# Hybrid trunk step on one core: seven-product in-projections in two blocks of layer B instead of three, and their summed weights prepared over two blocks

## The chip, the cores and the metric

The program runs on one core of one Trainium2 chip. The metric is the device time of one execution in microseconds, as the median of three runs.

## The reference, cut to what matters

One step of a two-layer decoder trunk over a prompt of 2048 tokens and a sample batch of 8 x 8 = 64 tokens, with model width 1024. Layer A is a gated delta rule; nothing of it changes. Layer B is a retention layer:

```python
def _ret_layer(x, pos0, S0, norm_w, w_in, onorm_w, w_out):
    B, L, _ = x.shape
    p = _rmsnorm(x, norm_w) @ w_in.astype(F32)
    q, k, v, gate = jnp.split(p, [B_QK, 2 * B_QK, 2 * B_QK + B_VW], axis=-1)
    q = _rotary(q.reshape(B, L, B_HEADS, B_DK), pos0)
    k = _rotary(k.reshape(B, L, B_HEADS, B_DK), pos0) * (B_DK ** -0.5)
    v = v.reshape(B, L, B_HEADS, B_DV)
    o, S = _retention_chunked(q, k, v, S0)
    o = _rmsnorm(o, onorm_w) * jax.nn.silu(gate.reshape(B, L, B_HEADS, B_DV))
    y = x + (o.reshape(B, L, B_VW) @ w_out.astype(F32)).astype(x.dtype)
    return y, S.astype(x.dtype)
```

There are 4 heads, with q and k of 256 and v and gate of 512 columns each. The in-projection `x @ w_in` is what the change computes in another way in one block of tokens.

## The kernel before, in words

**Tiling.** The prompt is cut into four blocks of 512 tokens (n = 0 to 3), and layer B runs over block and head (h = 0 to 3). Block 0 also carries the 64 sample tokens, so its tiles are 576 columns wide. For each head the loop computes gate, q, k and v, then starts the retention of that head as a background task (`ret_prompt`, four chunks of 128 tokens, and in block 0 `ret_sample` for the sample tokens), and then does the out-projection of the head before (`flush_B`, `outproj_B`). Every float32 product is done as three float32r matmuls on a high and a low half of each operand (`PASSES`); the halves of a weight tile come from an ACT cast and a DVE subtraction (`wload`, L196 and L197).

**Two ways to the in-projection.** The direct one (`colproj`, and the loop with `pv`) is used in block 0: for a head it takes 8 column tiles of 24 matmuls, and 96 matmuls for v, that is 288 matmuls of 512 columns where a block has 512 tokens. In block 0 a column tile of 576 columns is done as two pieces of 288. The seven-product one (`quad`, `vquad`, `seven`; Strassen's scheme in Winograd's form) is used in blocks 1 to 3: for a head four quads of 7 x 12 matmuls of 256 columns, and for v 7 x 24, that is 504 matmuls of 256 columns, with sums of the products on DVE and POOL. It needs summed activations (`build_halves`, built once per block) and summed weights.

**Preparing the summed weights.** `prep(u)` makes them: two generators (u = 0 and 1), each with 24 tiles (4 heads x 6 weight groups). A tile is four loads into `Rw` (L1038), four POOL sums into `Sm` (L1040 to L1043), an ACT cast back into `Rw` (L1045), a DVE subtraction (L1046) and two stores to the scratch tensors `wh_d` (L1049, L1050). `Rw` and `Sm` of one generator are the two buffers of one tag (`ta` for u = 0, `tb` for u = 1), so the loads of the next tile wait until the stores of the last have landed. `build_halves` uses the same two tags for `T2` and `T3`.

**What sets the order.** All loads and stores go through SP's one queue, in program order. Background tasks (`_Pipe`) are generators: the main code calls `pipe.pump()` after each group of matmuls, and a generator's next part is written out once the pipe's count of matmul time has passed the number of us that it yielded. Both `prep` generators start after q and k of head 0 of block 0. At the end of block 0, `pipe.wait(*ptask)` writes out all that is left of them before `build_halves`:

```python
            yield 6.0
            ...
            yield 4.5
            ACT.copy(R, Sm)
            V.tensor_tensor(Sm.bitcast(F32R), Sm, R.bitcast(F32), op=ALU.subtract)
            yield 3.0
```

```python
            if h == 3 and n + 1 < NB:
                pipe.wait(*ptask)
                xo = build_halves(n + 1, rb)
```

A tile framework then places the instructions of each engine; an engine works through its own list in order.

Of the kernel before, what the change touches and what calls it, by code (L numbers as in the profile page):

```python
# [10 lines left out]
F32 = mybir.dt.float32  # L11
F32R = mybir.dt.float32r
AF = mybir.ActivationFunctionType
ALU = mybir.AluOpType
# [77 lines left out]
def tile_hybrid(ctx: ExitStack, tc: tile.TileContext, a: dict, S: int):  # L92
# [929 lines left out]
    def halves_of(src, vkind, u):  # L1022
# [3 lines left out]
        return [src[j][:, 512 * i + 256 * u : 512 * i + 256 * u + 256] for j in range(2) for i in range(2)]  # L1026

    def prep(u):

        pb = B.pb  # L1030
        tag = ("ta", "tb")[u]
        for h, t in ((h, t) for h in range(BH) for t in range(6)):
            src, vkind = quads(h)[t]
            R = pb.tile([128, 4, 256], F32R, tag=tag, bufs=2, name="Rw")
            Sm = pb.tile([128, 4, 256], F32, tag=tag, bufs=2, name="Sm")
            A11, A12, A21, A22 = (R[:, i, :].bitcast(F32) for i in range(4))
            for x, y in zip((A11, A12, A21, A22), halves_of(src, vkind, u)):
                nc.sync.dma_start(x, y)  # L1038
            yield 6.0
            PL.tensor_tensor(Sm[:, 0], A21, A22, op=ALU.add)  # L1040
            PL.tensor_tensor(Sm[:, 1], Sm[:, 0], A11, op=ALU.subtract)  # L1041
            PL.tensor_tensor(Sm[:, 2], A11, A21, op=ALU.subtract)
            PL.tensor_tensor(Sm[:, 3], A12, Sm[:, 1], op=ALU.subtract)  # L1043
            yield 4.5
            ACT.copy(R, Sm)  # L1045
            V.tensor_tensor(Sm.bitcast(F32R), Sm, R.bitcast(F32), op=ALU.subtract)  # L1046
            yield 3.0
            out = wh_d[h][4 * t : 4 * t + 4].rearrange("x p (l v c) -> p x l v c", l=2, v=2)[:, :, :, u, :]
            nc.sync.dma_start(out[:, :, 0], R.bitcast(F32))  # L1049
            nc.sync.dma_start(out[:, :, 1], Sm)  # L1050
            yield 4.5

# [367 lines left out]
    for n in range(NB):  # L1420
        for h in range(4):
# [16 lines left out]
            if n:  # L1438
                S_ = pb.tile([128, 2, 512], F32, tag="Sr", bufs=2, name="Sr")
                nc.sync.dma_start(S_.rearrange("p k v -> p (k v)"), sr_d[h])  # L1440
                ws = wstream(h)
                for d in (0, 2):
# [5 lines left out]
            else:  # L1448
                ahead = []
                for d in range(4):  # L1450
                    if h == 0 and d == 0:
                        ahead = colproj2([wload(a["w_qkg"][16 + 4 * h + j]) for j in range(2)], xk, width)
                    pst = ahead.pop(0) if ahead else colproj(a["w_qkg"][16 + 4 * h + d], xk, width)
                    for p, s, e in pieces(pst, 0, TB):
                        ACT.activation(GT[:, d, s:e], p, AF.Silu)
                    V.tensor_scalar(GT[:, d, :], GT[:, d, :], onB[:, h, d : d + 1], None, op0=ALU.mult)
                    (p, _, _), = pieces(pst, TB, XC)
                    ACT.activation(GTs[:, d, :], p, AF.Silu)
                    V.tensor_scalar(GTs[:, d, :], GTs[:, d, :], onB[:, h, d : d + 1], None, op0=ALU.mult)
                    pipe.pump()  # L1460
            for kind in range(2):
                pair = []
                if n == 0:
                    for j in range(2):
                        pair.append(colproj(a["w_qkg"][kind * 8 + 2 * h + j], xk, width, (pp, po)[j]))
                        pipe.pump()
# [10 lines left out]
                else:  # L1477
                    KR = dst
                if n:
                    quad(ws, xo, dst)  # L1480
                    rope_in(dst, cs[:, 0], cs[:, 1])
                else:
                    rope(pair, cs[:, 0], cs[:, 1], [(lambda s, e, j=j: dst[:, j, s:e]) for j in range(2)], 0, TB)
                    for j in range(2):
                        (p, _, _), = pieces(pair[j], TB, XC)
                        ACT.copy(raws[:, kind, j], p)
                pipe.pump()
            if start:
# [3 lines left out]
                V.tensor_copy(GTs, Gs)  # L1492
                ptask = [pipe.add(prep(u), 9, lat=9.0 * u) for u in range(2)]
            if h == 3 and n + 1 < NB:
# [13 lines left out]
            Vt = pb.tile([128, 4, 512], F32, tag="Vt", name="Vt")  # L1508
            if n:
                vquad(ws, xo, Vt)  # L1510
            else:
                S_ = pb.tile([128, 2, 512], F32, tag="Sr", bufs=2, name="Sr")
                pv = [pp("pv"), pp("pv"), pp("pv"), po("pv")]
                pvs = po("pvs")
                for kp in range(4):
                    w = wload(a["w_v"][h, kp])
                    for kk in range(2):
# [5 lines left out]
                        for c, i in order:  # L1523
                            xl, wl = PASSES[i]
                            mm(pv[c], xn[k][:, xl, c * 128 : (c + 1) * 128], w[:, wl, wk],
                               start=(k == 0 and i == 0), stop=(k == 7 and i == 2))
                        for i, (xl, wl) in enumerate(PASSES):
                            mm(pvs[:64], xn[k][:, xl, TB:XC], w[:, wl, wk],
                               start=(k == 0 and i == 0), stop=(k == 7 and i == 2))
                        pipe.pump()  # L1530
                for c in range(4):
                    ACT.copy(Vt[:, c], pv[c])
                vraw = pb.tile([128, 512], F32, tag="p2", name="vraw")[:64]
                ACT.copy(vraw, pvs[:64])
            if h == 3 and n + 1 < NB:
                pipe.wait(*ptask)
                xo = build_halves(n + 1, rb)
            end = n == NB - 1 and h == 3
# [14 lines left out]

PIN = False
LAT_E = 4.0
LAT_SUB = 51.0
# [124 lines left out]
```

## Time and profile before

| what | value |
|---|---|
| runs | 3461.81, 3466.56, 3473.41 us, median 3466.56 |
| the profiled execution | 3472.95 us |
| its span on the core | 3471.0 us |
| TensorE (PE) matmul busy | 3214.7 us, 93% |
| DVE, ACT, POOL busy | 2393.1, 1578.0, 527.7 us |
| mean granted TensorE clock | 0.97 |

The span begins with the first instruction. Layer A and its start take the first 1447 us or so; block 0 of layer B runs from there to about 2124 us, then the three seven-product blocks follow. A time in us in the rows counts from the span's start. Matmuls overlap, so the busy time of a group says less than the distance from one start to the next. A wait names the engine that waited, the line, and what ended the wait. A granted clock of 1.00 is 2.4 GHz throughout, 0.50 is 1.2 GHz throughout.

### The profile page before, as it was taken

The page shows a single profiled execution, that of the slowest core. Times are in us where ns is not written, and L with a number is a line of the kernel's source. Part 1 is how long each engine was busy: PE and PEld are TensorE (multiplying, and loading weights), DVE is VectorE, ACT ScalarE, POOL GpSimd, SP SyncE. Part 2 cuts the span into 40 slices and gives each one's busy share as a digit, 9 for nine tenths or more (in the row PEclk, how much of TensorE's full clock was granted, in tenths as well). Part 3 has the DMA queues.
Part 4 walks back from the last instruction along what each step waited for, and adds up shares of the span by engine and source line. Part 5 has one row for each costly group of instructions (what it writes and reads, how often), then busy time and mean ns, then how long its engine had stood idle before and what let it go on. Part 6 is the DMA issues. An engine that isn't in the chain of part 4 may idle for free.

```text
span 3471.0 us, 59507 instructions
## 1 busy us (share of the span) xinstructions
PE 3214.7 (93%) x21436; PEld 2812.2 (81%) x21436; DVE 2393.1 (69%) x5358; ACT 1578.0 (45%) x3607; POOL 527.7 (15%) x810
## 2 busy tenths in 40 slices
PE   7999999999999999999989837999999999999997
PEld 6999777778687788877868627889989898889996
DVE  6876877787768878557566546576676666776666
ACT  7564664465435555334334333344443344533443
POOL 1211111001100000012323240111101111111110
PEclk9999999999999999999999968999999999999999
DMA  4333544435443342467778777887677867788675
GB/s 133 94 100 109 172 125 119 131 113 146 130 131 103 87 136 81 147 200 264 247 237 263 255 251 226 274 282 249 232 253 254 278 238 242 233 278 269 222 246 170
DMA packets 429014, 669.80 MB, mean 193 GB/s; under 512 B 121760, under 2 KB 245424, under 8 KB 428720
## 3 DMA queue, kind: packets, MB, share of 16 engines
q1 hardware_dynamic: 428720, 666.01, 59.5%
q8 instruction: 169, 2.77, 0.3%
q14 instruction: 125, 1.02, 0.1%
HBM read 517.08 MB, written 146.68 MB: 191 GB/s over the span
## 4 chain that ended last, share of the span: by engine, by line
PE 58%; DVE 12%; DMA 12%; ACT 6%; POOL 4%; issue 4%; SPq 2%; POOLq 0%; DVEq 0%; ACTq 0%
PE pp L101 32%; PE sq L101 7%; PE o L101 4%; DMA w<-wh_d 3%; PE sv L101 3%; PE p L101 3%; PE kyd L101 2%; PE oT L110 1%; DVE w L197 1%; DMA wraw<-in_w_v 1%; SPq L1038 1%; DMA wraw<-in_w_qkg 1%; POOL so L587 1%; POOL Sm L1041 1%; ACT w L196 1%
## 5 line engine op out<-in xcount | busy, mean ns | idle before, releaser
L101 PE MATMUL pp<-xn,w 128*128 128x288 f32 (+1 forms) x5456 | 1106.3, 350 | 38.2 <-ACT w L196 13.5
L101 PEld LDWEIGHTS pp<-xn,w 128*128 128x128 f32 x5456 | 857.5, 191 | 149.4 <-ACT w L196 16.5
L101 PE MATMUL pp<-OG,w 128*128 128x512 f32 (+1 forms) x2880 | 599.8, 367 | 38.0 <-DVE xr L1349 23.7
L101 PEld LDWEIGHTS pp<-OG,w 128*128 128x128 f32 x2880 | 494.8, 196 | 124.0 <-DVE xr L1349 22.2
L197 DVE TENSOR_TENSOR w<-wraw,w 128x1024 fp32r<-128x1024 f32 x272 | 344.4, 1268 | 91.6 <-ACT w L196 87.2
L196 ACT CAST w<-wraw 128x1024 fp32r<-128x1024 f32 x272 | 285.5, 1052 | 260.7 <-PE pp L101 108.5
L101 PE MATMUL sq<-xn,w 128*128 128x256 f32 x2304 | 309.9, 284 | 8.7 <-DVE GT L1116 3.7
L101 PEld LDWEIGHTS sq<-xn,w 128*128 128x128 f32 x2304 | 287.8, 188 | 15.8 <-issue 7.1
L210 ACT CAST w<-wraw 128x512 fp32r<-128x512 f32 x216 | 129.4, 623 | 220.6 <-PE pp L101 77.2
L211 DVE TENSOR_TENSOR w<-wraw,w 128x512 fp32r<-128x512 f32 x216 | 148.8, 703 | 61.8 <-ACT w L210 61.2
L1349 DVE TENSOR_TENSOR xr<-xr,pp 128x512 f32<-128x512 f32 (+1 forms) x160 | 92.1, 592 | 137.0 <-PE pp L101 122.6
L743 DVE SCALAR_TENSOR_TENSOR acc<-pp,cw,acc 128x511 f32<-128x511 f32 (+2 forms) x216 | 160.7, 744 | 21.0 <-ACT acc L740 20.8
L101 PE MATMUL sv<-w,xn 128*128 128x256 f32 x1152 | 146.3, 283 | 4.8 <-DMA w<-wh_d 4.7
L101 PEld LDWEIGHTS sv<-w,xn 128*128 128x128 f32 x1152 | 141.0, 189 | 7.4 <-DVE rt L1000 3.1
L1046 DVE TENSOR_TENSOR Sm<-Sm,Rw 128x1024 fp32r<-128x1024 f32 x48 | 61.3, 1278 | 85.6 <-ACT Rw L1045 48.1
L101 PE MATMUL p<-Vh,Kt 128*128 128x512 f32 x384 | 108.1, 411 | 6.7 <-ACT Kt L1185 5.6
L488 DVE TENSOR_TENSOR VP<-VP,tm 128x66 f32<-128x66 f32 (+26 forms) x510 | 107.5, 211 | 4.4
L486 DVE TENSOR_TENSOR tm<-LP,VP 128x66 f32<-128x66 f32 (+26 forms) x510 | 105.5, 207 | 6.1 <-DMA LP<-sl 2.1
L1045 ACT CAST Rw<-Sm 128x1024 fp32r<-128x1024 f32 x48 | 50.2, 1049 | 128.5 <-POOL Sm L1043 120.3
L101 PE MATMUL o<-Sc,Qc 128*128 128x512 f32 x360 | 101.5, 405 | 7.6 <-ACT Sc L210 5.8
L1161 POOL TENSOR_TENSOR so<-oss,rsc 128x1 f32<-128x1 f32 x72 | 18.0, 250 | 591.6 <-ACT on L1159 591.5
L210 ACT CAST OG<-og 128x256 fp32r<-128x256 f32 x192 | 71.7, 405 | 62.2 <-DVE og L1225 28.9
(434 smaller groups left out, 5775.0 us busy)
## 6 DMA issues: line engine op xcount, KB each, us to landing
w<-wh_d SPq DMA_DIRECT2D x288, 512.0 KB, 5.4
wraw<-in_w_in_a SPq DMA_DIRECT2D x128, 512.0 KB, 3.6
x_d<-xr SPq DMA_DIRECT2D x160, 256.0 KB, 3.5
wraw<-in_w_qkg SPq DMA_DIRECT2D x144, 256.0 KB, 4.4
xr<-x_d SPq DMA_DIRECT2D x128, 256.0 KB, 4.1
wraw<-in_w_out_b SPq DMA_DIRECT2D x64, 512.0 KB, 4.2
wh_d<-Rw SPq DMA_DIRECT2D x48, 512.0 KB, 3.4
wh_d<-Sm SPq DMA_DIRECT2D x48, 512.0 KB, 3.6
```

Source lines behind the costliest of these rows:

```text
L101: ins = nc.tensor.matmul(out, lhsT, rhs, start=start, stop=stop)
L110: ins = nc.tensor.transpose(out, x, ident[:p, :p])
L196: ACT.copy(w[:, 0, :], raw)
L197: V.tensor_tensor(w[:, 1, :], raw, w[:, 0, :].bitcast(F32), op=ALU.subtract)
L210: ACT.copy(hi, x)
L211: V.tensor_tensor(lo, x, hi.bitcast(F32), op=ALU.subtract)
L486: V.tensor_tensor(tv, LP[:, m, m + 1 : m + 1 + n].unsqueeze(2).to_broadcast([128, n, ncol]), VP[:, m, 0:ncol].unsqueeze(1).to_broadcast([1 ...
L488: V.tensor_tensor(VP[:, m + 1 : m + 1 + n, 0:ncol], VP[:, m + 1 : m + 1 + n, 0:ncol], tv, op=ALU.subtract)
L743: V.scalar_tensor_tensor(acc[:, sh:], ap[:, : TB - sh], cw[:, ct, j : j + 1], acc[:, sh:], op0=ALU.mult, op1=ALU.add)
L1045: ACT.copy(R, Sm)
L1046: V.tensor_tensor(Sm.bitcast(F32R), Sm, R.bitcast(F32), op=ALU.subtract)
L1349: V.tensor_tensor(xs[:, s:e], xs[:, s:e], p[:, : e - s], op=ALU.add)
```

## The change

A constant `FIRST7 = 2` is the first block with seven products. Block 1 takes the direct in-projection, without the sample columns, and `build_xn` in place of `build_halves`. The wait for the prepared weights moves from the end of block 0 to the end of block 1. The yields of `prep` become about twice as long (18 to 36 us of counted matmul time for a tile), and the second generator starts 18 instead of 9 us after the first. A new helper `behind()` ties the cast and the subtraction of a tile behind the last ACT and the last DVE instruction written out before them.

```diff
+    @contextmanager
+    def behind():
+
+        traced = nc.cur_bb.bb.instructions
+        with ExitStack() as st:
+            for e in (ACT, V):
+                st.enter_context(tc.issue_after(next(i for i in reversed(traced) if i.engine == e.engine)))
+            yield
...
-            yield 6.0
+            yield 10.0
...
-            yield 4.5
-            ACT.copy(R, Sm)
-            V.tensor_tensor(Sm.bitcast(F32R), Sm, R.bitcast(F32), op=ALU.subtract)
-            yield 3.0
+            yield 10.0
+            with behind():
+                ACT.copy(R, Sm)
+                V.tensor_tensor(Sm.bitcast(F32R), Sm, R.bitcast(F32), op=ALU.subtract)
+            yield 8.0
...
-            yield 4.5
+            yield 8.0
...
+            if n >= FIRST7:
                 ws = wstream(h)
...
-                if n == 0:
+                if n < FIRST7:
                     for j in range(2):
                         pair.append(colproj(a["w_qkg"][kind * 8 + 2 * h + j], xk, width, (pp, po)[j]))
...
-                if n:
+                if n >= FIRST7:
                     quad(ws, xo, dst)
...
-                ptask = [pipe.add(prep(u), 9, lat=9.0 * u) for u in range(2)]
+                ptask = [pipe.add(prep(u), 9, lat=18.0 * u) for u in range(2)]
...
-            if n:
+            if n >= FIRST7:
                 vquad(ws, xo, Vt)
...
             if h == 3 and n + 1 < NB:
-                pipe.wait(*ptask)
-                xo = build_halves(n + 1, rb)
+                if n + 1 < FIRST7:
+                    xn = build_xn(x1_d, n + 1, 1, rb, TB)
+                else:
+                    pipe.wait(*ptask)
+                    xo = build_halves(n + 1, rb)
...
+FIRST7 = 2
```

What the diff leaves out here are the conditions `if samp` around the sample columns of gate, q, k and v in the direct path.

Where the instructions then stand, in three places around the wait for the prepared weights. In the names, `Rw` and `Sm` are the two tiles of `prep`, `wh_d_76` the scratch tensor of head 3, `xr` and `x_d` the running sum of the out-projection, `OG` its input, `Vh`, `Kt`, `Ah`, `Sc`, `Qc`, `on` tiles of the retention, and `rmk` the retention's decay mask.

SP's queue before, at the end of block 0, from the loads of the out-projection's weights on:

```order
L195 DMA wraw<-in_w_out_b 128x1024 x2
L1049 DMA wh_d_76<-Rw 128x4x256
L1050 DMA wh_d_76<-Sm 128x4x256
L1049 DMA wh_d_76<-Rw 128x4x256
L1050 DMA wh_d_76<-Sm 128x4x256
L1038 DMA Rw<-in_w_qkg 128x256 x8
L195 DMA wraw<-in_w_out_b 128x1024 x2
L1049 DMA wh_d_76<-Rw 128x4x256
L1050 DMA wh_d_76<-Sm 128x4x256
L1049 DMA wh_d_76<-Rw 128x4x256
L1050 DMA wh_d_76<-Sm 128x4x256
L1038 DMA Rw<-in_w_qkg 128x256 x8
```

SP's queue now, at the end of block 1, from the last loads of the out-projection's weights on:

```order
L195 DMA wraw<-in_w_out_b 128x1024 x3
L1059 DMA wh_d_76<-Rw 128x4x256
L1060 DMA wh_d_76<-Sm 128x4x256
L1059 DMA wh_d_76<-Rw 128x4x256
L1047 DMA Rw<-in_w_qkg 128x256 x4
L1060 DMA wh_d_76<-Sm 128x4x256
L1047 DMA Rw<-in_w_v 128x256 x4
L1360 DMA x_d<-xr 128x512
L1059 DMA wh_d_76<-Rw 128x4x256
L1060 DMA wh_d_76<-Sm 128x4x256
L1059 DMA wh_d_76<-Rw 128x4x256
L1047 DMA Rw<-in_w_v 128x256 x4
```

Before, from this place on, ten of the 48 tiles of `prep` had still to be stored; the loads of two tiles follow each two pairs of stores, and two of the four loads of the out-projection's weights, and behind them the mask `rmk` of the last head, stood among them. Now seven tiles have still to be stored, loads and stores alternate tile by tile, and the four loads of the out-projection's weights and the mask (16 rows ahead of this piece) stand in front.

ACT's list before, at the end of block 0, behind the last copies of v out of the PSUM banks:

```order
L1534 COPY vraw<-pvs 64x512
L210 CAST xn_21877<-xt 128x256
L210 CAST xn_21877<-xs 128x256
L1185 ACTIVATE Kt<-kT,rsc 128x256
L1045 CAST Rw<-Sm 128x1024 x2
L196 CAST w<-wraw 128x1024 x2
L1045 CAST Rw<-Sm 128x1024 x2
L196 CAST w<-wraw 128x1024
L1045 CAST Rw<-Sm 128x1024
L210 CAST Sc<-Sr 128x512
L1045 CAST Rw<-Sm 128x1024 x3
L210 CAST Ah<-A 128x128
```

ACT's list now, at the end of block 1, from the last copies of v on:

```order
L1545 COPY Vt<-pv 128x512 x3
L1055 CAST Rw<-Sm 128x1024 x2
L196 CAST w<-wraw 128x1024 x2
L1055 CAST Rw<-Sm 128x1024
L1195 ACTIVATE Kt<-kT,rsc 128x256
L1055 CAST Rw<-Sm 128x1024
L210 CAST Ah<-A 128x128
L210 CAST Qc<-QR 128x256
L1169 ACTIVATE on,oss<-o 128x512
```

Of the 48 casts `Rw<-Sm`, 38 stood ahead of the last copies of v of block 0, and ten behind. Now 20 stand ahead of the last copies of v of block 0, 21 between those and the last of block 1, and seven behind, among the retention of the last head.

PE's list now, at the end of block 1, from the last of a run of 60 out-projection matmuls behind v to the first of the retention's last head:

```order
L101 MATMUL pp<-OG_24985,w 128x512 x6
L101 MATMUL pp<-OG_24986,w 128x512 x6
L110 MATMUL kT<-ident,KR 128x128 x2
L101 MATMUL ap<-QR,KR 128x128 x2
L101 MATMUL o<-Sc,Qc 128x512 x6
L101 MATMUL p<-Vh,Kt 128x512 x2
L101 MATMUL o<-Vh,Ah 128x512 x2
```

The last rows ahead of the first seven-product matmuls of block 2:

```order
L101 MATMUL pp<-OG_24986,w 128x512 x6
L101 MATMUL pp<-OG_24985,w 128x512 x6
L101 MATMUL pp<-OG_24986,w 128x512 x6
L101 MATMUL sq<-xn_25802,w 128x256 x6
L101 MATMUL sq<-xn_25803,w 128x256 x6
L101 MATMUL sq<-xn_25802,w 128x256 x6
```

Before, 36 of the 192 out-projection matmuls of 288 columns stood ahead of the retention's last head there and 156 behind it. Now 60 of the 96 of 512 columns stand ahead, and 36 behind.

## Rows read from the trace of the kernel before

**Rows 1.** Page: busy time of each engine; the chain that ended last.

```profile
PE 3214.7 (93%) x21436; PEld 2812.2 (81%) x21436; DVE 2393.1 (69%) x5358; ACT 1578.0 (45%) x3607; POOL 527.7 (15%) x810
...
PE 58%; DVE 12%; DMA 12%; ACT 6%; POOL 4%; issue 4%; SPq 2%; POOLq 0%; DVEq 0%; ACTq 0%
```

**Rows 2.** Windows: block 0 (two), its end, block 1's first, last head; block 2.

```profile
core 0: us, PE busy (x) PEld busy (x) DVE busy (x) ACT busy (x) POOL busy (x), PEclk, DMA share, GB/s
1447.00:1709.00 262.00, 248.01 (x1490) 215.75 (x1489) 153.21 (x263) 95.73 (x188) 61.20 (x81) 0.98 0.66 217
1709.00:2008.00 299.00, 254.99 (x1482) 215.31 (x1480) 189.11 (x311) 118.86 (x237) 96.16 (x118) 0.93 0.77 253
2008.00:2124.00 116.00, 51.79 (x258) 43.83 (x259) 56.44 (x98) 35.18 (x66) 36.28 (x46) 0.67 0.71 225
2124.00:2249.00 125.00, 114.97 (x825) 102.86 (x824) 74.74 (x134) 47.85 (x96) 11.29 (x16) 0.97 0.83 274
2462.00:2575.00 113.00, 107.93 (x726) 97.72 (x725) 86.78 (x169) 53.01 (x114) 12.51 (x18) 0.98 0.71 239
2575.00:2996.00 421.00, 408.51 (x2812) 375.06 (x2812) 289.20 (x525) 180.64 (x369) 54.27 (x74) 1.00 0.74 251
```

**Rows 3.** Timeline of PE: v of block 0, first quad of block 1 (start, us, ...).

```profile
2000.18 2.96 PE L101 MATMUL pv<-w,xn 128*128 128x512 f32 x12
2002.98 0.86 PE L101 MATMUL pvs<-w,xn 128*64 128x512 f32 x3
...
2123.73 3.03 PE L101 MATMUL sq<-xn,w 128*128 128x256 f32 x24
2126.60 1.56 PE L101 MATMUL sq<-ta,w 128*128 128x256 f32 x12
```

**Rows 4.** Groups of PE, 2008 to 2124 us, then 1709 to 2008 (last row).

```profile
L101 PE MATMUL pp<-OG,w 128*128 128x288 f32 x192 | 31.8, 334 | 20.6 <-DVE xr L1349 14.9 <-ACT w L196 5.6
L101 PE MATMUL p<-Vh,Kt 128*128 128x512 f32 x15 | 7.3, 569 | 5.9 <-ACT Kt L1185 5.6 <-DVE Kt L1186 0.3
L101 PE MATMUL o<-Sc,Qc 128*128 128x512 f32 x15 | 6.3, 498 | 5.0 <-ACT Sc L210 4.4 <-DVE Sc L211 0.5
L101 PE MATMUL o<-Vh,Ah 128*128 128x512 f32 x9 | 4.2, 569 | 1.2 <-ACT Ah L210 1.2
...
L101 PE MATMUL pp<-OG,w 128*128 128x288 f32 x192 | 26.8, 299 | 0.1
```

**Rows 5.** Waits, 2008 to 2124 us: total, times, longest.

```profile
PE ap L101 <- DVE A L1193: 33.4, 1, 33.4
...
PE pp L101 <- DVE xr L1349: 14.9, 1, 14.9
```

**Rows 6.** Timeline of SP's queue: one round of two tiles, start of the next.

```profile
2018.83 4.66 SPq L1038 DMA_DIRECT2D Rw<-in_w_qkg  x8
...
2027.88 0.38 SPq L1049 DMA_DIRECT2D wh_d<-Rw  x1
...
2032.97 0.36 SPq L1050 DMA_DIRECT2D wh_d<-Sm  x1
2033.37 4.66 SPq L1038 DMA_DIRECT2D Rw<-in_w_qkg  x8
```

**Rows 7.** Timeline of ACT: last copy of v; last cast, last activation split.

```profile
2005.38 1.06 ACT L1532 COPY Vt<-pv 128x512 f32<-128x512 f32 x2
...
2078.24 1.04 ACT L1045 CAST Rw<-Sm 128x1024 fp32r<-128x1024 f32 x1 [1.74 <-POOL Sm L1043]
...
2098.25 0.41 ACT L210 CAST tc<-xs 128x256 fp32r<-128x256 f32 x1 [0.50 <-DVE xs L1104]
```

**Rows 8.** Waits of PE and ACT in the second half of block 0, 1709 to 2008 us.

```profile
PE pp L101 <- ACT w L196: 13.2, 3, 6.0
...
PE pp L101 <- ACT GT L1455: 5.4, 3, 2.9
...
ACT Rw L1045 <- POOL Sm L1043: 53.3, 17, 8.2
```

More of the change, by code (lines that the diff above doesn't have):

```diff
@@ L1 @@
 import math
-from contextlib import ExitStack
+from contextlib import ExitStack, contextmanager
 import numpy as np
@@ L1456, in tile_hybrid @@
                     V.tensor_scalar(GT[:, d, :], GT[:, d, :], onB[:, h, d : d + 1], None, op0=ALU.mult)
-                    (p, _, _), = pieces(pst, TB, XC)
-                    ACT.activation(GTs[:, d, :], p, AF.Silu)
-                    V.tensor_scalar(GTs[:, d, :], GTs[:, d, :], onB[:, h, d : d + 1], None, op0=ALU.mult)
+                    if samp:
+                        (p, _, _), = pieces(pst, TB, XC)
+                        ACT.activation(GTs[:, d, :], p, AF.Silu)
+                        V.tensor_scalar(GTs[:, d, :], GTs[:, d, :], onB[:, h, d : d + 1], None, op0=ALU.mult)
                     pipe.pump()
@@ L1483, in tile_hybrid @@
                     rope(pair, cs[:, 0], cs[:, 1], [(lambda s, e, j=j: dst[:, j, s:e]) for j in range(2)], 0, TB)
-                    for j in range(2):
+                    for j in range(2 if samp else 0):
                         (p, _, _), = pieces(pair[j], TB, XC)
@@ L1508, in tile_hybrid @@
             Vt = pb.tile([128, 4, 512], F32, tag="Vt", name="Vt")
-            if n:
+            if n >= FIRST7:
                 vquad(ws, xo, Vt)
             else:
-                S_ = pb.tile([128, 2, 512], F32, tag="Sr", bufs=2, name="Sr")
+                if n == 0:
+                    S_ = pb.tile([128, 2, 512], F32, tag="Sr", bufs=2, name="Sr")
                 pv = [pp("pv"), pp("pv"), pp("pv"), po("pv")]
-                pvs = po("pvs")
+                pvs = po("pvs") if samp else None
                 for kp in range(4):
@@ L1526, in tile_hybrid @@
                                start=(k == 0 and i == 0), stop=(k == 7 and i == 2))
-                        for i, (xl, wl) in enumerate(PASSES):
+                        for i, (xl, wl) in enumerate(PASSES if samp else ()):
                             mm(pvs[:64], xn[k][:, xl, TB:XC], w[:, wl, wk],
@@ L1532, in tile_hybrid @@
                     ACT.copy(Vt[:, c], pv[c])
-                vraw = pb.tile([128, 512], F32, tag="p2", name="vraw")[:64]
-                ACT.copy(vraw, pvs[:64])
+                if samp:
+                    vraw = pb.tile([128, 512], F32, tag="p2", name="vraw")[:64]
+                    ACT.copy(vraw, pvs[:64])
             if h == 3 and n + 1 < NB:
-                pipe.wait(*ptask)
-                xo = build_halves(n + 1, rb)
+                if n + 1 < FIRST7:
[3 more added lines that the diff above has]
+                    xo = build_halves(n + 1, rb)
             end = n == NB - 1 and h == 3
```

## The prediction

> **What bounds the kernel now.** I read the page first, then a table of stretches, then the stretches themselves. The page shows PE busy for 93% of the span and 58% of the chain that ended last [rows 1], so TensorE sets the time wherever it is fed, and the question is where it is not. The table of stretches answers that [rows 2]: block 2 of layer B runs 421 us with 408.5 us of matmuls at clock 1.00, as full as this kernel gets. Block 0 does not: its second half has 299 - 255 = 44 us without a matmul and a clock of 0.93, and the 116 us at its end hold 51.8 us of matmuls at a mean granted clock of 0.67, which is two thirds of that stretch at 1.2 instead of 2.4 GHz. That end is a drain: the last tiles of summed weights are finished while PE has little left. Its waits name it: 33.4 us for the masked product A, whose mask load stands on SP behind the loads and stores of `prep`, and 14.9 us for the out-projection's addition [rows 5].
>
> I sum against the profiled execution, 3472.95 us with a span of 3471.0. It lies 6.4 us above the median of 3466.56, and the result is carried over to the median. A measurement of this kernel can tell about 0.3%, some 10 us, from no change.
>
> **Block 1's in-projection, directly.** Twelve matmuls of 512 columns start within 2002.98 - 2000.18 = 2.80 us, so 0.233 us each; 24 of 256 columns within 2126.60 - 2123.73 = 2.87 us, so 0.1196 us each [rows 3]. A head costs 288 x 0.233 = 67.1 us directly and 504 x 0.1196 = 60.3 us by seven products. The difference of 6.8 us falls on PE, which is the bound there, four times: **+27 us**. The sums of products and the sets of summed activations go from DVE and POOL in this block; both are below 70% and 14% busy in block 2 [rows 2], so that earns nothing by itself. The weight splits now go through ACT and DVE as in block 0, whose first half kept PE busy for 248 of 262 us with them and with `prep` beside [rows 2].
>
> **The drain at the end of block 0 goes.** It lasts 116 us [rows 2]. What PE does in it would take, fed steadily, 26.8 us for the 192 out-projection matmuls (the last of rows 4 has them in a full stretch) and 39 x 0.233 = 9.1 us for the retention matmuls of 512 columns [rows 4], some 36 us. So about 80 us are lost, clock included. The next loads there are those of `build_xn`, which need no prepared weights. The nearest row for an ordinary end of a block is block 1's last head, 113 us with 107.9 busy and clock 0.98 [rows 2]: 5 us idle and 2 us of clock. I take 12 us, because the retention of the sample tokens lies just behind: **-68 us**. Bounds: -50, if the outgoing sample work or the single buffer of the activations holds PE, and -75.
>
> **A drain at the end of block 1 comes.** The order shows seven tiles behind the last copies of v, where there were ten. A round of two tiles takes 2033.37 - 2018.83 = 14.5 us on SP's queue: eight loads, then two pairs of stores, each waiting for its cast [rows 6]. The first two casts stand right behind the copies, at some 4 us, and the seventh three rounds later, at 4 + 3 x 14.5 = 48 us. Before, the last of the ten was at 2078.2, 72 us behind the last copies from 2005.4 on, and the splits of the summed activations ended at 2098.7, another 20 us later, because they need the buffers of `prep` [rows 7]. So the first seven-product matmul comes at about 48 + 20 = 68 us. Until then PE has 96 x 0.233 = 22 us of out-projection, 60 of the 96 ahead of the retention by the order, and 60 x 0.233 = 14 us of retention: 36 us, and nothing else. That leaves 32 us idle. The old drain did 36 us of matmuls in 51.8 busy us [rows 2, 4], since the clock fell to half in it; I add 8 us for that and subtract the 7 us of an ordinary end: **+33 us**. Bounds: 0, if the casts end within the cover, and +70, as long as the old one.
>
> **Less in PE's way in block 0.** In its second half ACT waited 53.3 us in 17 places for POOL's sums of `prep`, with everything behind it on its list; PE waited 13.2 us for weight casts and 5.4 us for gates [rows 8]. The second half lost 44 us idle and 0.07 x 299 = 21 us of clock, 65 us. The nearest row with the same sample work and no `prep` is the first head of block 1: 10 us idle and 4 us of clock, so 28 us for two heads [rows 2]. The 37 us between them are what `prep` costs there. The first half lost 14 us and 5 of clock, no more than that row, so nothing is to be gained there. By the order 20 tiles instead of 38 stand in block 0, and the casts come 10 instead of 4.5 us of counted time behind the sums and behind other work: I take two thirds, **-24 us** (bounds 0 and -37).
>
> **`prep` in block 1.** The other 21 tiles lie in block 1, which had none. It has the sample work only in its first head. **+10 us** (bounds 0 and +37, block 0's old price).
>
> The longer yields and the pair of edges of `behind()` add no instruction, and the 48 tiles and their 192 loads and 96 stores stay the same, only spread: their cover is SP's slack in block 1, which moves less, since 24 loads of summed weights per head go. Were that slack gone, SP's waits would show as the bounds of the last two terms.
>
> The sum is 27 - 68 + 33 - 24 + 10 = **-22 us**: 3451 for an execution like the profiled one, **3444** as a median.
>
> **A rule that says otherwise.** The rows give 233 and 120 ns a matmul, close to proportional to the columns [rows 3]. The Trainium skill (TensorE: Matmul & The Clock Gate, Back-to-back issue gap) states sustained gaps of about 131 ns for 512 columns and 81 for 128, which would put 256 at an estimated 98; by that page's figures a direct head costs 37.7 us against 49.4 and block 1 gains 47 us instead of losing 27. The trace disagrees for these float32r matmuls, with its 233 and 120.
>
> **Rivals.**
>
> *The new drain is as long as the old one (slower).* Each store waits on SP for a cast that is now tied behind a retention instruction, which itself waits for PE; loads and stores now alternate tile by tile, so two tiles no longer overlap as in rows 6. For it: the casts of the last five tiles stand among the retention. Against it: the mask and the out-projection's weights are ahead this time, so PE's 36 us cannot be held as in rows 5. Price: 70 instead of 33, -22 + 37 = +15 us, 3482. It decides once seven tiles take 85 us instead of 48, which is 27 us a round.
>
> *The contention only moves (no change).* Block 1 gets block 0's old 37 us, and block 0 keeps a third more. For it: 21 tiles in four heads are more than half the old density, and PE's direct weights need ACT and DVE in time. Against it: block 0's first half at full density lost next to nothing. Price: +27, so +5 us, 3472.
>
> *The new drain is covered.* Nothing of the 33 remains. For it: 36 us of work for 48 us of tiles. Against it: the splits of 20 us come only behind the last tile. Price: -55 us, 3412.
>
> *Spacing by weight loads and not by columns.* If 512 columns could follow each other as fast as 256 do, at 0.1196 us, a direct head would cost 34.4 us against 60.3, and block 1 gain 103 us: -22 - 27 - 103 = -152, 3315. Rows 3 speak against it in block 0's own matmuls.
>
> *The change does not do what it says.* The order shows the 20, 21 and 7 tiles and the direct matmuls in block 1, so this gets no chance of its own.
>
> **How the numbers follow.** The forecast gets 0.47, the new drain as long as the old one 0.19, the contention that moves 0.18, the covered drain 0.14, the spacing by weight loads 0.01, and 0.01 is for nothing listed. Faster by over 10 us are the covered drain, the other spacing and most of the forecast's own spread (0.40 of 0.47), with a little of the moved contention: 0.58. Within 10 us are most of the moved contention and the rest of the forecast: 0.20. Slower is the long drain, with a little beside it: 0.22. The range reaches from 3400, somewhat under the covered drain, to 3488, somewhat over the long one; terms at their bounds together lie outside.
>
> **What would show it.** In the profile of the changed kernel: no stretch near 2010 us with PE under 85%; one such stretch, 60 to 80 us long, at the end of block 1, some 430 to 470 us later, with clock under 0.9 and waits for `prep` or for splits; block 1 at some 450 to 500 us without that stretch; ACT's waits for POOL's sums in the second half of block 0 well below 53.3 us; blocks 2 and 3 unchanged at 421 us each. The forecast is wrong if the new stretch exceeds 100 us, or if block 1's heads show PE waiting for weight casts as block 0 did.

## The result and the profile after

The changed kernel takes 3383.95 us (median of 4 runs, 3382.75 to 3395.24) against 3466.73 us (4 runs) of the kernel before: a ratio of 0.976, 95% interval 0.974 to 0.978. The forecast of 3444 us, with its range from 3400 to 3488, has the sign right and the size wrong: the kernel gained 83 us where 22 were forecast, and the result lies below the range.

The profiled execution took 3395.24 us, with a span of 3393.5, so it lies 11 us above its median. The sum below compares it with the profiled execution of before: -77.5 us of span. Its page has this busy time and this chain [rows 1]:

```profile
PE 3216.8 (95%) x20572; PEld 2769.3 (82%) x20572; DVE 2357.0 (69%) x5218; ACT 1563.8 (46%) x3527; POOL 493.7 (15%) x770
...
PE 66%; DVE 10%; DMA 10%; ACT 6%; issue 4%; POOL 3%; SPq 1%; DVEq 0%; POOLq 0%; ACTq 0%
```

The windows of the changed kernel answer to [rows 2]: the two halves of block 0, its end, block 1 up to the last copies of v, the end of block 1, block 2, and block 3 to the end.

```profile
core 0: us, PE busy (x) PEld busy (x) DVE busy (x) ACT busy (x) POOL busy (x), PEclk, DMA share, GB/s
1441.00:1693.00 252.00, 241.93 (x1489) 210.90 (x1488) 143.56 (x259) 90.89 (x182) 40.30 (x58) 1.00 0.60 195
1693.00:1951.00 258.00, 244.82 (x1479) 207.74 (x1479) 175.54 (x302) 111.76 (x228) 56.05 (x74) 0.99 0.71 228
1951.00:1996.00 45.00, 42.65 (x267) 38.12 (x265) 19.96 (x35) 11.88 (x20) 7.43 (x10) 1.00 0.77 246
1996.00:2428.00 432.00, 419.77 (x1950) 335.82 (x1949) 283.10 (x421) 184.70 (x324) 91.05 (x117) 0.99 0.68 221
2428.00:2508.00 80.00, 46.75 (x183) 35.08 (x183) 50.71 (x86) 30.73 (x61) 20.33 (x26) 0.77 0.68 220
2508.00:2918.00 410.00, 399.68 (x2759) 367.22 (x2758) 276.70 (x499) 170.48 (x343) 52.15 (x68) 1.00 0.77 256
2918.00:3394.00 476.00, 448.79 (x2993) 406.84 (x2991) 309.85 (x544) 194.75 (x393) 58.38 (x82) 0.98 0.70 235
```

The stretches of the kernel before that [rows 2] lack are block 0 as a whole, block 1 as a whole, and block 3 to the end:

```profile
1447.00:2007.00 560.00, 503.00 (x2970) 431.05 (x2968) 341.32 (x573) 213.59 (x422) 157.35 (x198) 0.95 0.72 236
2124.00:2575.00 451.00, 428.12 (x2943) 387.03 (x2942) 298.35 (x544) 184.29 (x378) 54.20 (x73) 0.99 0.78 260
2996.00:3471.00 475.00, 447.33 (x2995) 405.91 (x2993) 310.07 (x544) 194.38 (x393) 58.15 (x82) 0.99 0.70 236
```

The low clock is gone from the end of block 0 (45 us at 1.00 where 116 stood at 0.67) and has come, weaker, to the end of block 1 (80 us at 0.77). What the prediction watched for is there: one such stretch, and that at the end of block 1. What it did not expect, or not at this size, stands in the other rows: block 0 fell by 50 us and block 2 by 11, and block 1, with its 4 x 288 direct matmuls and 21 tiles of `prep`, took 432 us up to its last copies of v, where the whole of it had taken 451.

The new drain goes as forecast up to the end of the splits. ACT's timeline in it, from the last copies of v, over the last cast of `prep`, to the last activation split:

```profile
2426.83 1.56 ACT L1545 COPY Vt<-pv 128x512 f32<-128x512 f32 x3
...
2472.86 1.04 ACT L1055 CAST Rw<-Sm 128x1024 fp32r<-128x1024 f32 x1 [2.15 <-POOL Sm L1052]
...
2493.56 0.40 ACT L210 CAST tc<-xs 128x256 fp32r<-128x256 f32 x1 [0.50 <-DVE xs L1114]
```

PE's timeline in it (start, length, operation, count, and in brackets the idle time and what ended it):

```profile
2427.58 14.13 PE L101 MATMUL pp<-OG,w 128*128 128x512 f32 x60
...
2470.76 1.95 PE L101 MATMUL o<-Sc,Qc 128*128 128x512 f32 x3 [2.72 <-ACT Sc L210]
2495.19 11.47 PE L101 MATMUL pp<-OG,w 128*128 128x512 f32 x36 [22.48 <-DVE xr L1359]
2506.49 3.00 PE L101 MATMUL sq<-xn,w 128*128 128x256 f32 x24
```

The last cast of `prep` starts at 2472.9, 46 us behind the start of the copies of v at 2426.8, where 48 had been worked out. The splits end 21 us later (20 forecast). The 36 held-back out-projection matmuls, which the forecast had counted among the work that covers the drain, then come ahead of the first `sq`, so that this starts 80 us behind the copies, and not 68. PE's longest idle time, 22.5 us, is the wait for DVE's out-projection addition, which stands behind the splits of the summed activations on DVE's list.

### The profile page after: what moved, and what is told of

It reads as the page before. It is cut to its first block, busy times and chain, and to the rows that moved or that the text cites. A ratio compares the mean times of both kernels' runs of the same rounds, so it can differ in the third digit from the quotient of the medians.

```text
span 3393.5 us, 57080 instructions
## 1 busy us (share of the span) xinstructions
PE 3216.8 (95%) x20572; PEld 2769.3 (82%) x20572; DVE 2357.0 (69%) x5218; ACT 1563.8 (46%) x3527; POOL 493.7 (15%) x770
## 4 chain that ended last, share of the span: by engine, by line
PE 66%; DVE 10%; DMA 10%; ACT 6%; issue 4%; POOL 3%; SPq 1%; DVEq 0%; POOLq 0%; ACTq 0%
PE pp L101 37%; PE sq L101 5%; PE pv L101 5%; PE o L101 4%; PE p L101 4%; PE sv L101 3%; PE kyd L101 2%; DMA w<-wh_d 1%; DMA wraw<-in_w_qkg 1%; PE oT L110 1%; DMA x_d<-xr 1%; DVE w L197 1%; DMA wraw<-in_w_v 1%; POOL so L587 1%; DMA out_ret_s<-st 1%
## 5 line engine op out<-in xcount | busy, mean ns | idle before, releaser
L101 PE MATMUL pp<-xn,w 128*128 128x288 f32 (+1 forms) x6224 | 1285.6, 354 | 12.6 <-ACT xn L210 4.7
L101 PEld LDWEIGHTS pp<-xn,w 128*128 128x128 f32 x6224 | 993.4, 189 | 156.2 <-issue 19.3
L196 ACT CAST w<-wraw 128x1024 fp32r<-128x1024 f32 x320 | 336.6, 1052 | 383.6 <-PE pp L101 201.5
L197 DVE TENSOR_TENSOR w<-wraw,w 128x1024 fp32r<-128x1024 f32 x320 | 403.0, 1260 | 149.9 <-ACT w L196 141.0
L101 PE MATMUL sq<-xn,w 128*128 128x256 f32 x1536 | 206.2, 284 | 5.8 <-DVE GT L1126 3.3
L101 PEld LDWEIGHTS sq<-xn,w 128*128 128x128 f32 x1536 | 191.4, 188 | 10.4 <-issue 3.8
L101 PE MATMUL pv<-w,xn 128*128 128x512 f32 x768 | 188.5, 398 | 1.9 <-ACT w L196 1.7
L101 PEld LDWEIGHTS pv<-w,xn 128*128 128x128 f32 x768 | 144.2, 189 | 39.5 <-ACT w L196 1.9
L211 DVE TENSOR_TENSOR w<-wraw,w 128x512 fp32r<-128x512 f32 x144 | 96.9, 688 | 46.7 <-ACT w L210 46.6
L110 PE MATMUL oT<-ident,on 128*128 128x128 f32 x432 | 74.7, 280 | 26.8 <-DVE on L588 11.8
```

What stands on the lines that cost most here:

```text
L101: ins = nc.tensor.matmul(out, lhsT, rhs, start=start, stop=stop)
L110: ins = nc.tensor.transpose(out, x, ident[:p, :p])
L196: ACT.copy(w[:, 0, :], raw)
L197: V.tensor_tensor(w[:, 1, :], raw, w[:, 0, :].bitcast(F32), op=ALU.subtract)
L211: V.tensor_tensor(lo, x, hi.bitcast(F32), op=ALU.subtract)
```

## The experiments

All kernels below start from the changed one. Medians are of four runs beside runs of the kernel before on the same chip (medians 3469 to 3475 us); where one run is named, there is no interval. A stretch's length comes from the profiled execution: "block 0" runs from its first gate to its last copies of v, "block 1" from its first gate to the same place, and an end of a block from there to the first gate or first `sq` of the next. Lengths are rounded by themselves, so they can differ by one from those of the windows shown, which are cut at whole us.

**Theories.** The forecast missed by 55 us in the profiled execution. *Waiting for sums*, the prediction's own: block 0 loses because ACT stands waiting for POOL's sums, and the helper `behind()` cures this. *Density*: block 0 loses by the number of tiles of `prep` in it, whatever waits for what. Within density, the price can be the bytes moved, SP's time to issue them, SP held by stores that wait, or the sums and casts. And for block 1, either a direct block costs 27 us more than one of seven products, as forecast, or it doesn't.

### The parts of the change

Four kernels change the pace or the helper:

```diff
# e1_pace31: a slightly denser pace (each yield of 10.0, each of 8.0)
-            yield 10.0
+            yield 8.5
-            yield 8.0
+            yield 7.0
-                ptask = [pipe.add(prep(u), 9, lat=18.0 * u) for u in range(2)]
+                ptask = [pipe.add(prep(u), 9, lat=15.5 * u) for u in range(2)]
# e3_oldpace: the old pace (yields 6.0, 4.5, 3.0, 4.5), with behind()
-                ptask = [pipe.add(prep(u), 9, lat=18.0 * u) for u in range(2)]
+                ptask = [pipe.add(prep(u), 9, lat=9.0 * u) for u in range(2)]
# e2_only_first7: as e3_oldpace; e4_nobehind: the new pace; both without behind()
-            with behind():
-                ACT.copy(R, Sm)
-                V.tensor_tensor(Sm.bitcast(F32R), Sm, R.bitcast(F32), op=ALU.subtract)
+            ACT.copy(R, Sm)
+            V.tensor_tensor(Sm.bitcast(F32R), Sm, R.bitcast(F32), op=ALU.subtract)
```

> The change with the old yields and without the edges behind other work: only the first seven-product block moves. By the order 36 casts stand in block 0 and all 48 ahead of the end of block 1's first head. Theory A (prep at full pace costs block 0 about 50 us of PE time, of which half the pace and the edges took nearly all): block 0 as before, 50 us more, the drain of 33 us gone, so 17 us more than the change, 3401, range 3392 to 3410. Rival (block 0's second half was slow before because the end of the block drew tiles and the loads of the next block into it): block 0 within 15 us of the change's, total 3351 to 3366.

> The change with the old yields, but with the edges of behind(). By the order 36 casts stand in block 0, 46 ahead of the end of block 1's first head. If the density of tiles does it (36 instead of 20 in block 0), as the run with neither: 3392 to 3410, block 0 some 45 us longer than in the change. If the place of the casts on ACT's and DVE's lists does it, so that ACT no longer waits for POOL's sums: block 0 within 15 us of the change's, no drain, 3351 to 3368.

> The change without the edges of behind(), with the long yields. By the order the casts then stand earlier: 31 in block 0, 45 ahead of the end of block 1's second head, 48 ahead of its third's, though the generators write them out at the slow pace. If density does it, block 0 takes back two thirds of the 50 us and the drain of 33 us goes: 3375 to 3390. If the place of the casts does it, the same by another way, with ACT's waits for POOL's sums back at some 50 us or more in block 0. If neither matters: 3351.

> The change with shorter yields in prep (8.5, 8.5, 7, 7 instead of 10, 10, 8, 8; second generator 15.5 instead of 18 later). By the order 22 casts stand in block 0 and all 48 ahead of the last copies of v of block 1. Theory D (the drain at the end of block 1 costs about 33 us net, since PE is idle there for 33 us and at a low clock for some more): 33 us less than the change, 3351, range 3345 to 3360, and no stretch near 2430 us with PE under 90%. Rival (PE's idle time there comes from the splits of the summed activations and from the out-projection's additions behind them on DVE, not from prep): at most 10 us less, 3374 to 3384, with the hole still there.

| kernel | median, us | ratio, 95% | block 0 | its end | block 1 | its end | blocks 2, 3 |
|---|---|---|---|---|---|---|---|
| changed | 3383.95 | 0.974 to 0.978 | 509 | 45 | 432 | 79 | 887 |
| e2_only_first7 | 3417.58 | 0.981 to 0.988 | 555 | 62 | 433 | 24 | 896 |
| e3_oldpace | 3408.79 | 0.979 to 0.986 | 557 | 55 | 434 | 24 | 895 |
| e4_nobehind | 3380.23 | 0.971 to 0.977 | 528 | 49 | 439 | 24 | 899 |
| e1_pace31 | 3358.58 | 0.966 to 0.972 | 506 | 43 | 444 | 24 | 896 |

The old pace brings block 0 back to 555 and 557 us (560 before), without the helper and with it; e2_only_first7 came out somewhat slower than density had it. ACT's waits for POOL's sums, which the prediction took for the sign of the loss [rows 8], don't go with it. ACT in block 0 of the kernel before, then of e2_only_first7, old pace without the helper (total, times, longest):

```profile
ACT Rw L1045 <- POOL Sm L1043: 77.2, 26, 8.2
```

```profile
ACT Rw L1054 <- POOL Sm L1052: 60.3, 22, 7.0
```

Of e3_oldpace, old pace with it:

```profile
ACT w L196 <- DMA wraw<-in_w_v: 34.4, 7, 9.4
...
ACT Rw L1055 <- POOL Sm L1052: 17.5, 7, 3.2
```

and of e4_nobehind, new pace without it:

```profile
ACT Rw L1054 <- POOL Sm L1052: 64.8, 23, 5.9
```

So e3_oldpace has rid ACT of most of these waits and keeps the slow block: ACT waits longer for raw weights instead, 34.4 us for those of v against 19.0 in e2_only_first7. And e4_nobehind has 64.8 of the 77.2 us of before and a block some 30 us shorter. Waiting for sums falls, density stands. What the helper does at the new pace is to keep the tiles where the yields put them: by the order of instructions, 31 casts stand ahead of block 0's last copies of v without it, 20 with it, and 48 instead of 41 ahead of block 1's. That is why e4_nobehind has no drain at the end of block 1, and its time is that of the changed kernel all the same.

e1_pace31 shows what the new drain costs, since with 22 tiles in block 0 all 48 are done ahead of block 1's last copies of v. The end of block 1 falls from 79 to 24 us; block 1 takes 12 us more with its 26 tiles instead of 21, and blocks 2 and 3 take 9 us more, because the changed kernel does the last head's retention in the drain and not in block 2 (2759 matmuls stand in its block 2, 2836 here). Windows of e1_pace31 (blocks 0 and 1 with their ends, blocks 2 and 3):

```profile
1443.00:1950.00 507.00, 487.24 (x2966) 418.97 (x2965) 324.88 (x564) 202.70 (x412) 105.02 (x139) 0.99 0.67 221
1950.00:1992.00 42.00, 41.04 (x261) 37.36 (x261) 21.14 (x35) 13.38 (x22) 9.24 (x13) 1.00 0.83 269
1992.00:2461.00 469.00, 448.74 (x2061) 357.61 (x2060) 310.40 (x473) 198.60 (x351) 99.13 (x127) 0.98 0.70 230
2461.00:2882.00 421.00, 412.02 (x2836) 377.59 (x2835) 291.54 (x529) 181.58 (x372) 54.68 (x74) 1.00 0.75 253
2882.00:3357.00 475.00, 448.48 (x2992) 407.39 (x2991) 308.95 (x544) 194.19 (x393) 58.26 (x82) 0.98 0.70 236
```

### No seven products at all

```diff
-FIRST7 = 2
+FIRST7 = 4
-                ptask = [pipe.add(prep(u), 9, lat=18.0 * u) for u in range(2)]
```

> All four blocks directly, no prep at all: the floor of block 0 without any tile, and what seven products are worth in blocks 2 and 3. If a block is worth the 27 us of its matmul count, 55 us more than the run with the shorter yields, less some 10 us each for the tiles gone from blocks 0 and 1: 3393, range 3380 to 3410, with block 0 at 490 to 500 us between its first gate and its last copies of v (509 in the change, 560 before). Rival (the sums and the weight transfers of the seven-product blocks eat what they save): 3360 or less.

It takes 3346.51 us (3337.47 to 3353.66; the best of the kernels above had 3358.58), a ratio of 0.964 with an interval from 0.961 to 0.966. The rival was right: this is the fastest kernel of the study, though its interval just touches that of e1_pace31. Its windows are block 0 and its end, block 1 up to the last copies of v, its end, block 2, and block 3 to the end:

```profile
1451.00:1943.00 492.00, 480.81 (x2960) 416.58 (x2959) 282.02 (x541) 183.48 (x389) 21.03 (x46) 1.00 0.49 157
1943.00:1986.00 43.00, 41.31 (x262) 37.48 (x261) 19.15 (x35) 11.87 (x20) 0.73 (x2) 1.00 0.56 180
1986.00:2402.00 416.00, 413.64 (x1955) 334.57 (x1955) 249.90 (x400) 166.94 (x302) 16.65 (x37) 1.00 0.50 158
2402.00:2440.00 38.00, 38.00 (x171) 30.90 (x170) 18.48 (x28) 11.81 (x21) 0.73 (x2) 1.00 0.60 194
2440.00:2873.00 433.00, 432.96 (x1953) 351.10 (x1952) 250.56 (x387) 166.88 (x290) 13.95 (x34) 1.00 0.45 143
2873.00:3352.00 479.00, 460.80 (x2085) 373.04 (x2083) 271.98 (x428) 180.71 (x320) 16.18 (x40) 0.99 0.42 137
```

It gives four prices. Block 0 without `prep` takes 492 us, so the 38 tiles cost 560 - 492 = 68 us and the 20 tiles of the changed kernel 510 - 492 = 18. Block 2 in the direct way takes 433 us, against 421 by seven products. Block 1 takes 416 + 38 = 454 us, against 451. And the whole of seven products, as e1_pace31 has them: `prep` costs it 507 - 492 = 15 us in block 0 and 469 - 454 = 15 in block 1, and blocks 2 and 3 earn 12 and 4.

PE in block 2 is busy 433.0 of 433 us here and 408.5 of 421 in the kernel before [rows 2]. The direct matmuls cost 24.5 us more, about as forecast (27), but half of what seven products save is lost again, because their block leaves PE idle for 12.5 us. The largest of its waits (kernel before, block 2) are these:

```profile
PE sv L101 <- DMA w<-wh_d: 4.7, 5, 1.9
PE pp L101 <- DVE xr L1349: 2.5, 2, 2.1
PE sq L101 <- DMA w<-wh_d: 1.1, 2, 0.6
```

For the kernel without seven products the trace lists no wait of PE in block 2.

### What about `prep` costs block 0

Six kernels take all blocks the direct way, so that the prepared weights are not used and only block 0 and what lies just behind it differ. They go at the old pace; n3_nostore has the helper, the others not. One run each.

```diff
# n1_full: all of prep
-FIRST7 = 2
+FIRST7 = 4
# n2_dmaonly: loads and stores without the sums, the cast and the subtraction
-            PL.tensor_tensor(Sm[:, 0], A21, A22, op=ALU.add)
...
-            nc.sync.dma_start(out[:, :, 1], Sm)
+            nc.sync.dma_start(out[:, :, 1], R.bitcast(F32))
# n3_nostore: without the stores
-            nc.sync.dma_start(out[:, :, 0], R.bitcast(F32))
-            nc.sync.dma_start(out[:, :, 1], Sm)
# n4_tiny: as n2_dmaonly, 16 of 256 columns in each load and store
-                nc.sync.dma_start(x, y)
+                nc.sync.dma_start(x[:, :16], y[:, :16])
# n5_poolq: as n2_dmaonly, on POOL's queue
-                nc.sync.dma_start(x, y)
+                PL.dma_start(x, y)
# n6_nohold: as n2_dmaonly, one pair of tiles for good, made ahead of the loop; stores of zeros
+        R = pb.tile([128, 4, 256], F32R, tag=tag, bufs=2, name="Rw")
+        Sm = pb.tile([128, 4, 256], F32, tag=tag, bufs=2, name="Sm")
+        PL.memset(Sm, 0.0)
...
-            R = pb.tile([128, 4, 256], F32R, tag=tag, bufs=2, name="Rw")
-            Sm = pb.tile([128, 4, 256], F32, tag=tag, bufs=2, name="Sm")
-            nc.sync.dma_start(out[:, :, 0], R.bitcast(F32))
+            nc.sync.dma_start(out[:, :, 0], Sm)
```

> All four blocks directly, prep at the old pace without the edges, its output unused: 36 tiles in block 0. The seven-product blocks are not there to help or harm, so block 0 shows the price of the tiles alone: 50 us more than in the run without prep, 540 to 560 us for block 0.

> As n1_full, but each tile is only loaded and stored (the sums, the cast and the subtraction are left out; the loaded values are stored twice): the same 36 tiles, loads and stores, on SP's queue and the DMA engines in block 0. If the queue and the transfers are the price of a tile, block 0 keeps 35 us or more of the 50: 530 us or more. If the work on POOL, ACT and DVE is it, block 0 lies within 15 us of the run without prep.

> As n1_full with the edges of behind(), but without the two stores of a tile: 36 tiles with loads, sums, cast and subtraction in block 0. The stores are what makes SP's queue stand still until a cast is done. If that is the price, block 0 lies within 20 us of the run without prep; if the work of the engines is it, it keeps 35 us or more of the 50.

> As n2_dmaonly with the same number of loads and stores at the same places, but each moves 16 of 256 columns (the tiles are not the ones that seven products would need, and no product reads them). If the bytes on the DMA engines are the price of the 36 tiles in block 0, block 0 falls from 527 to within 10 us of the 492 of the run without prep. If it is the issue on SP's one queue and the standing still there, it stays above 515.

> As n2_dmaonly, but the loads and stores of the tiles are issued from POOL's queue, so that SP's queue holds nothing of prep; the bytes are the same. If SP's queue is the price, block 0 falls to within 12 us of 492; if the bytes are, it stays above 515.

> The kernel with only the loads and stores of the summed weights (none of them is used: all blocks take the direct way, so no output depends on them), at the dense pace, but with nothing on SP's queue that waits: each generator keeps one pair of tiles for good, the loads go into the one, and the stores take constant zeros from the other, so no store waits for a load and no load for a store. The same bytes, the same 72 or so stores and some 150 loads in block 0. Theory bytes (they delay the weight loads and the loads of the sample state beside them): block 0 stays at 515 us or more, near the 527 of the kernel whose stores wait, and loads of raw weights land in about 5.4 us. Rival, SP held (a store that waits for its four loads, or a load that waits for a store, keeps the weight loads behind it on SP): block 0 falls to 505 us or less, near the 492 without any preparation. Between 505 and 515 both have a share. Whole time: 3392 or more for bytes, 3370 or less for the held queue.

| kernel | time, us | block 0 | above 492 | MB moved in block 0 | landing of q, k, gate weights, us |
|---|---|---|---|---|---|
| n0_none7 | 3346.51 | 492 | 0 | 77 | 3.6 |
| n1_full | 3446.39 | 555 | 63 | 131 | 5.0 |
| n2_dmaonly | 3404.22 | 527 | 35 | 132 | 5.4 |
| n3_nostore | 3373.72 | 512 | 20 | 97 | 4.2 |
| n4_tiny | 3355.25 | 495 | 3 | 82 | 3.8 |
| n5_poolq | 3441.18 | 587 | 95 | 153 | 4.9 |
| n6_nohold | 3409.01 | 530 | 38 | 132 | 5.7 |

(The MB of n0_none7 are its 157 GB/s times 492 us; the others stand in the trace's DMA view.) Block 0 of n2_dmaonly and of n6_nohold, in the windows' columns:

```profile
1443.00:1970.00 527.00, 493.66 (x2963) 424.62 (x2962) 280.67 (x540) 181.90 (x389) 23.72 (x84) 0.97 0.76 250
```

```profile
1443.00:1973.00 530.00, 496.46 (x2963) 426.31 (x2962) 281.64 (x540) 181.77 (x389) 22.50 (x48) 0.97 0.76 249
```

What n6_nohold waits for there, on PE and on ACT:

```profile
ACT w L196 <- DMA wraw<-in_w_qkg: 35.5, 7, 9.9
...
ACT w L196 <- DMA wraw<-in_w_v: 27.5, 10, 6.8
...
PE os L101 <- DMA st<-in_state_ret: 9.6, 3, 4.5
...
PE pp L101 <- ACT w L196: 7.5, 4, 2.8
```

Loads and stores alone cost block 0 some 35 us of the 63. With all 192 loads and 96 stores in block 0, at a sixteenth of the size, 3 us are left, so it is not SP's time to issue them, nor the number of packets (some 117,000 there and 97,000 in n6_nohold). With one pair of tiles for good it is 38 us, so it is not SP held by a store either. In the trace of n6_nohold the stores of `prep` wait on SP's queue for 2 us in all, and its loads for 14, none of them over 1.1 at a time. n2_dmaonly had hardly more (3 and 17 us), so it had already shown the same. What is left are the bytes: in n6_nohold they fill the 16 DMA engines to 76% on average at 249 GB/s, where n0_none7 has 49% at 157. A 512 KB load of raw weights then lands in 5.4 to 5.7 instead of 3.6 to 3.9 us, and ACT, which casts them, waits 35.5 and 27.5 us for them. Of the 38 us, 22 are more idle time of PE and 16 are longer busy time, at a granted clock of 0.97 instead of 1.00. Most of those bytes are stores: without them, and with the sums and casts in, 20 us are left. The other 28 us of n1_full over n2_dmaonly go with the sums, casts and subtractions between the transfers. SP held by a store is open again for these 28, since stores now wait for casts and subtractions; SP in block 0 of n1_full:

```profile
SPq L1058 <- ACT Rw L1054: 38.5, 13, 4.5
...
SPq L1059 <- DVE Sm L1055: 10.7, 10, 2.0
```

Against it stands that the same two waits add up to more in the changed kernel (24.9 and 7.1 us) than in e4_nobehind (13.2 and 7.8), whose block 0 is 19 us longer. The runs don't split these 28 us.

n5_poolq was to take the held queue away as well. It says less than n6_nohold, since it did not keep the number of tiles: all 48 fell into block 0 and not some 36, the DMA engines were 78% busy, and block 0 became slower still, at 587 us.

The same move was tried where it could have been of use, with e1_pace31's pace, which keeps the number of tiles alike:

```diff
# e5_poolq, against e1_pace31; the same for the two stores
-                nc.sync.dma_start(x, y)
+                PL.dma_start(x, y)
```

> The run with the shorter yields (3358.6 us), with the loads and stores of prep on POOL's queue. If SP's queue is what the tiles cost, block 0 goes from 506 to some 495 and block 1 from 444 to some 425: 3325 to 3340, which would beat the run without seven products (3346.5). If the bytes cost it, 3350 to 3365. A third way, slower than 3370: POOL's own issue holds up its sums and the retention's small POOL steps.

It takes 3408.02 us, a ratio of 0.982 with an interval from 0.979 to 0.986: 49 us more than e1_pace31, all of it in block 0 (556 against 506) with 22 tiles in each. It is the third way of its expectation, slower than 3370. The Trainium skill (DMA: Bandwidth & Descriptors, Issuing engines are not separate DMA queues) says that transfers started by ScalarE, SyncE or GpSimd run on the same 16 DMA engines and interleave. The trace agrees so far as that nothing was relieved: PE's waits for loads of the sample state, which stayed on SP, went from 3.9 to 25.2 us. Here are that wait in block 0 of e1_pace31, and PE's longest waits in block 0 of e5_poolq:

```profile
PE os L101 <- DMA st<-in_state_ret: 3.9, 3, 2.2
```

```profile
PE os L101 <- DMA st<-in_state_ret: 25.2, 6, 5.5
PE pp L101 <- DVE xr L1359: 12.2, 6, 5.1
```

Why it is worse than on SP, and not equal, stays open. Fewer bytes a second went through (203 against 221 GB/s), so here it isn't their amount. POOL was busy 188.9 instead of 105.0 us, its DMA instructions among that, and the stores held POOL for 46.5 us in wait for casts, with the sums of the retention's norm behind them, for which ACT waited 21.1 instead of 11.2 us. The transfers issued on POOL are also of another kind: the trace has them in a queue called software_dynamic, and SP's in one called hardware_dynamic. No run separates these.

## Why the prediction was wrong, step by step

Each step against what was measured, in profiled executions:

| step | forecast | measured | from |
|---|---|---|---|
| the drain at the end of block 0 goes | -68 | -72 | 117 (2007 to 2124 us) to 45 |
| a drain at the end of block 1 comes | +33 | +31 | 80, less 38 for the end of block 1 in n0_none7, less the 11 by which block 2 is shorter |
| `prep` in block 1 | +10 | +16 | 432, less 416 in n0_none7 |
| block 1's in-projection, directly | +27 | +3 | 454 in n0_none7, less 451 |
| less in PE's way in block 0 | -24 | -50 | 560 to 510 |
| layer A, block 3 | 0 | -5 | 1441 and 476, against 1447 and 475 |
| sum | -22 | -77 | |

Three steps hold. The old drain was worth what was worked out. The new one also is, although by two misses that cancel: it is 12 us longer than forecast, and the block behind it is 11 us shorter. Neither of the rivals on it (as long as the old one, or covered) came true, nor did the contention that only moves: block 1 lost 17 us, idle and clock together, with 21 tiles in it. (The price given for that rival, +27 us, also leaves out the third more that it says block 0 keeps.)

**First failed step: less in PE's way in block 0, -24 us with bounds 0 and -37.** The size, 37 us, was the 65 us of idle time and clock in the second half, less a baseline of 28 us for two heads from block 1's first head, "the nearest row with the same sample work and no `prep`". That head is no clean baseline: it stands behind a drain and is itself a seven-product head, with its own waits. n0_none7 has the clean one: block 0 without `prep` loses 492 - 481 = 11 us in all, so the tiles cost 68 us and not 37. The first half wasn't free either: it fell from 262 to 252 us. And the mechanism was another one. ACT's 53.3 us of waits for POOL's sums did fall as forecast, to 1.4 us in the second half, but by luck beside the gain: e3_oldpace took most of them away and block 0 gained nothing. The price hangs on how many tiles share the stretch, and grows faster than their number: 38 cost 68 us, 1.8 each, the 31 of e4_nobehind 36, and 20 cost 18, 0.9 each. Half the pace thus gives back three quarters. The bytes of the loads and stores make up some 35 us of the 63 that 36 tiles cost in n1_full; what makes up the rest stays open. Two thirds of the right price would have been -45.

**Second failed step: block 1's in-projection, +27 us.** The 6.8 us a head are matmul time, and that was right: PE is busy 452 us in block 1 of n0_none7 and 428 in that of before, 24 us more. The sentence that failed is that the sums and the summed activations "go from DVE and POOL in this block" and that this "earns nothing by itself", because both are far from full. PE idled for 451 - 428 = 23 us in block 1 of before, in many short waits for streamed weights, for splits and for additions, and for 2 us in the direct one. The step counted what PE does and not what it waits for. It was also the one term of the sum without bounds; a lower bound from the window of block 1 before, 27 - 23 = 4 us, was there to be read.

These two missed by 26 and 24 us, nearly all of the 55. Layer A's 6 us lie within what its end varies between the runs of the study, whose block 0 begins at 1435 to 1451 us. The last 5 us between the executions' difference (77.5) and the medians' (82.8) come from the places of the two profiled executions above their medians, 6 and 11 us.

*Spacing by weight loads* had 0.01 and falls by the same rows: the direct block 2 is full at 433 us, 12 us more than by seven products, where that rival needs it to be 103 us less. The Trainium skill's gap of about 131 ns for 512 columns (TensorE: Matmul & The Clock Gate, Back-to-back issue gap) would make it 47 us less by the estimate that the prediction had from it. The trace does not agree, with 24 us more of matmul time.

## What to carry to other kernels

Price a scheme that saves matmuls by the length of a whole steady block either way, idle time and the preparing of its operands included: here the seven products save 24 us of matmuls a block, give 12 of them back in waits, and need 48 tiles which, at the best pace tried, cost 30 us, where two blocks earn 16. Take the price of background work from a stretch that has none of it, not from the waits it shows: an engine that waits for it may cost nothing, and its bytes may cost more than half. And when background transfers delay the loads that feed the bound engine, spread them; nearly halving their number in block 0 took three quarters of the price away.

## What the runs showed of the hardware

- Background transfers slow loads before the DMA engines are full on average: with the mean busy share of the 16 engines at 76% instead of 49% (90% or more in 13 of 40 slices of block 0 instead of none), a 512 KB weight load landed in 5.4 to 5.7 instead of 3.6 to 3.9 us, and block 0 took 38 us longer (n6_nohold against n0_none7).
- The number of transfers mattered little: 192 loads and 96 stores of a sixteenth of the size cost 3 us in the same block, although the DMA engines' mean busy share there was 61% (n4_tiny).
- Moving plain loads and stores from SP's to POOL's queue made a kernel 49 us slower (e5_poolq against e1_pace31), with fewer GB/s moved.
